# A shift moved from a row of maxima into the exponential's bias, and one cast moved from VectorE to ScalarE, in an attention and retention block

## Chip, cores and metric

The kernel runs on one core of a Trainium2 chip. The metric is the device time of one execution in microseconds (us), the median of several runs. TensorE (PE) multiplies matrices and writes to PSUM, VectorE (DVE) and ScalarE (ACT) read PSUM and SBUF, GpSimd (POOL) works on SBUF alone, and SyncE (SP) issues the DMAs. Each engine runs its own instructions in program order and waits on semaphores for the others.

## What is computed

A block of a streaming encoder over 4096 positions of width 1024: an RMS norm, one input projection, two groups of heads, a gated mix, an output projection, a second norm and the residual sum. The first group is forgetting attention, 8 heads of width 64; the second is chunkwise retention, 4 heads of width 128. What the change touches is the softmax of the attention:

```python
logits = jnp.einsum('bhqd,bhkd->bhqk', qb, kb) * scale
logits = logits + c[:, :, q0:q1, None] - c[:, :, None, :q1]
logits = jnp.where(kpos <= qpos, logits, -jnp.inf)
p = jax.nn.softmax(logits, axis=-1)
outs.append(jnp.einsum('bhqk,bhkd->bhqd', p.astype(vb.dtype), vb))
```

A softmax does not change when one constant is added to all logits of a row. The kernel subtracts a rough maximum of each row and adds a constant shift, so that the exponentials fit their 16-bit type.

## The kernel before

**Stages.** `phase_f0` (0 to about 425 us) norms the input, splits it into two 16-bit parts and projects the first four attention heads. Then `attention` runs over 64 items, one per head and block of 512 queries (`items`, head by head, 8 blocks each). Beside it run the fillers (`fill_f1`, `fill_r` twice, `fill_o`): the projections of the other heads, the retention and the output projection. A loop at the end of the kernel interleaves the two by their costs. After the last item `fill_o` runs alone to the end.

**A step of attention.** An item has 4 to 32 steps, one per 128 keys; over all items that is 1152. In a step TensorE forms 128 x 512 logits in a PSUM bank with two matmuls (the first also adds the row's negative maximum, which lies as rows 0 to 16 of the tile `xq`). ScalarE takes the exponential twice, in float32 (`pf`, line 1132) and in float16 (`ph`, line 1133), both with the scale `es`, an operand of one value per partition from the tile `gsc`. GpSimd forms the rest `pl = pf - ph` (line 308). The step then waits in the list `pvq`; `emit_pv` multiplies `ph` and `pl` by the values, four steps at a time, once at least six are queued.

**Maxima.** `max_tile` forms one tile of logits a second time, 128 queries by 512 keys, without the forget terms, and VectorE takes the maximum along the keys (line 999, tile `mrow`): 1152 tiles too. With the last tile of an item `max_row` starts. It reduces to one value per query (line 1011, tile `m4`, named `sm` in the trace), adds the shift (a `tensor_scalar` at line 144), waits `MAGE` ticks, transposes on TensorE (line 1017), lets ScalarE cast the coarse part (`mr[:, 0]`, line 1019), lets VectorE form what is left (line 147) and cast it as the second part (`mr[:, 1]`, line 144), and sends both through DRAM (`MR`) into `xq`.

**What sets the order.** The order on every queue is written by the program: each helper is a generator that is resumed once per `tick()`, and a `yield` inside it moves what follows one tick later. Ticks come with every step of attention and every step of a filler. Line 144 is the helper `ts`, line 141 `tt`, line 147 `stt`, line 308 the GpSimd helper, line 104 `mm` and line 107 the DMA helper, so tiles tell instructions apart better than lines. All PSUM tiles share one pool of 8 banks.

```python
        yield 1
        ts(m4, m4, gsc[items[n][0] // 4][0][:, KT + 5 : KT + 6], None, ALU.add, ALU.bypass)
        for _ in range(MAGE):
            yield 1
```

Of the kernel before, what the change touches and what calls it, by code (L numbers as in the profile page):

```python
# [12 lines left out]
AF = mybir.ActivationFunctionType  # L13
ALU = mybir.AluOpType
# [3 lines left out]
KT = 8  # L18
# [2 lines left out]
NEG = -1.0e30  # L21
NORM_EPS = 1e-6
GN_EPS = 1e-5
PSHIFT = 24.0
CP = 16
R1 = CP + 1
R2 = R1 + CP + 2
TOP, MID, LOW = 2.0**15, 2.0**9, 2.0**-2
# [25 lines left out]
def kernel(  # L54
# [14 lines left out]
    nc = tc.nc  # L69
# [18 lines left out]
    def SB(tag, shape, dt=F32):  # L88
        cnt[0] += 1
        slot = SHARED.get(tag, tag)  # L90
        return sbp.tile(shape, dt, tag=slot, name=f"{tag}_{cnt[0]}", bufs=BUFS.get(slot, 1))

    def PS():
        cnt[0] += 1
        return psp.tile([128, 512], F32, tag="ps", name=f"ps_{cnt[0]}", bufs=8)
# [7 lines left out]
    def mm(o, lhsT, rhs, start, stop):  # L103
        nc.tensor.matmul(out=o, lhsT=lhsT, rhs=rhs, start=start, stop=stop, skip_group_check=True)  # L104

    def dma(o, i):
        nc.sync.dma_start(out=o, in_=i)  # L107
# [18 lines left out]
    def until(key):  # L126

        while key not in done:
            assert chains, key
            tick()  # L130
# [9 lines left out]
    def tt(o, a, b, op):  # L140
        nc.vector.tensor_tensor(out=o, in0=a, in1=b, op=op)  # L141

    def ts(o, a, s1, s2, op0, op1):
        nc.vector.tensor_scalar(out=o, in0=a, scalar1=s1, scalar2=s2, op0=op0, op1=op1)  # L144

    def stt(o, a, s, b, op0, op1):
        nc.vector.scalar_tensor_tensor(out=o, in0=a, scalar=s, in1=b, op0=op0, op1=op1)  # L147
# [24 lines left out]
    gain = SB("gain", [128, KT])  # L172
    fbb = SB("fbb", [128, FH])
    nhalf = SB("nhalf", [128, 4])
    gsc = [[SB(f"gsc{g}{part}", [128, KT + 8]) for part in range(2)] for g in range(5)]
    state = [SB(f"state{h}", [128, 5, 128]) for h in range(2)]

# [49 lines left out]
    def w_scale(g, parts, mk, age=VAGE):  # L227

        n = KT * len(parts)
        m1 = SB("sm", [128, 1])  # L230
        if g < 4:
            for i in range(len(parts)):
                tt(mk[:, i * KT : (i + 1) * KT], mk[:, i * KT : (i + 1) * KT], gain, ALU.mult)
        nc.vector.tensor_reduce(out=m1, in_=mk[:, 0:n], axis=AX.X, op=ALU.max, apply_absolute_value=True)
        for _ in range(age):
            yield 1
        p = PS()
        nc.tensor.transpose(p[0:1, 0:128], m1, idf)
        m2 = SB("sm", [1, 1])
        nc.vector.tensor_reduce(out=m2, in_=p[0:1, 0:128], axis=AX.X, op=ALU.max)  # L240
        ts(m2, m2, 1e-6, 1.0 / 8192.0, ALU.max, ALU.mult)
        for _ in range(age):
            yield 1
        p2 = PS()
        mm(p2[:, 0:1], tri[0:1, :], m2, True, True)
        sc = SB("sm", [128, 1])
        nc.vector.reciprocal(out=sc, in_=p2[:, 0:1])
        for part in parts:
            f = gsc[g][part]
            if g < 4:  # L250
                ts(f[:, 0:KT], gain, sc[:, 0:1], None, ALU.mult, ALU.bypass)
            else:
                ts(f[:, 0:KT], gain, 0.0, sc[:, 0:1], ALU.mult, ALU.add)
            ts(f[:, KT : KT + 1], p2[:, 0:1], 1.0 / 512.0, None, ALU.mult, ALU.bypass)
        yield 1
        for part in parts:
            f = gsc[g][part]
            ts(f[:, KT + 1 : KT + 2], f[:, KT : KT + 1], 0.5, None, ALU.mult, ALU.bypass)
            if g < 2 and part == 0:


                ts(f[:, KT + 3 : KT + 4], sc, 1.0 / 512.0, 16.0, ALU.mult, ALU.min)
                tt(f[:, KT + 2 : KT + 3], f[:, KT + 3 : KT + 4], f[:, KT : KT + 1], ALU.mult)
                tt(f[:, KT + 3 : KT + 4], f[:, KT + 3 : KT + 4], f[:, KT + 3 : KT + 4], ALU.mult)
                ts(f[:, KT + 5 : KT + 6], f[:, KT + 3 : KT + 4], PSHIFT, None, ALU.mult, ALU.bypass)
                ts(f[:, KT + 6 : KT + 7], f[:, KT + 3 : KT + 4], 8.0, None, ALU.mult, ALU.bypass)
                ts(f[:, KT + 7 : KT + 8], f[:, KT + 3 : KT + 4], -8.0, None, ALU.mult, ALU.bypass)
                nc.vector.reciprocal(out=f[:, KT + 4 : KT + 5], in_=f[:, KT + 6 : KT + 7])
            elif g < 4:
                stt(f[:, KT + 2 : KT + 3], f[:, KT : KT + 1], 131072.0, f[:, KT : KT + 1], ALU.mult, ALU.mult)  # L270
            else:
                ts(f[:, KT + 2 : KT + 3], sc, 1.0, None, ALU.mult, ALU.bypass)
            done.add(("ws", g, part))
# [264 lines left out]

    def phase_f0():
        nc.vector.memset(nhalf, -0.5)  # L540
        wu = SB("z1", [128, 512], BF16)
        nc.gpsimd.memset(wu, 0.0)
        xs = a_load(0, 0, 2, "xt")
# [366 lines left out]
    items = [(h, qb) for h in range(FH) for qb in range(NB)]  # L910
# [98 lines left out]
    def max_row(n, xq, mrow, qb):  # L1009
        m4 = SB("sm", [128, 4])  # L1010
        nc.vector.tensor_reduce(out=m4, in_=mrow[:, :, 0 : qb + 1], axis=AX.X, op=ALU.max, negate=True)
        yield 1
        ts(m4, m4, gsc[items[n][0] // 4][0][:, KT + 5 : KT + 6], None, ALU.add, ALU.bypass)
        for _ in range(MAGE):
            yield 1
        p = PS()
        nc.tensor.transpose(p[0:4, 0:128], m4, idf)
        mr = SB("mr", [4, 2, 128], F16)
        nc.scalar.activation(out=mr[:, 0, :], in_=p[0:4, 0:128], func=AF.Copy, scale=1.0 / (TOP * CP))
        yield 1  # L1020
        r = SB("sm", [4, 128])
        stt(r, mr[:, 0, :], -TOP * CP, p[0:4, 0:128], ALU.mult, ALU.add)
        ts(mr[:, 1, :], r, 1.0 / MID, None, ALU.mult, ALU.bypass)
        for _ in range(3):
            yield 1
        dma(MR[n].rearrange("w (t p) -> t w p", p=128), mr)
        for _ in range(4):
            yield 1
        dma(xq[0:CP, :], MR[n][0:1, :].to_broadcast([CP, 512]))
        dma(xq[CP:R1, :], MR[n][1:2, :])  # L1030
        done.add(("m", n))
# [3 lines left out]
    def attention():  # L1035
# [65 lines left out]
        for n, (h, qb) in enumerate(items):  # L1101
            xq = xqs.pop(n)
            lq, z = lqs.pop(n)
            it = dict(n=n, z=z)
            es = gsc[h // 4][0][:, KT + 4 : KT + 5]
            until(("m", n))
            steps = 4 * (qb + 1)
            for kt in range(steps):
                c, kk = kt // 4, kt % 4
                kc, vt = get_chunk(h, c)  # L1110
                chunks_use[n, kt] = (kc, vt)
                cost = 0.0
                if kt % 2 == 0:
                    if kt % 4 == 2 and len(pvq) >= 6:
                        for _ in range(4):
                            cost += 88 * (4 - max(0, pvq[0][2]))
                            emit_pv()
                    sts = []
                    for j in (kt - 4 * qb, kt + 1 - 4 * qb):
                        p = PS()  # L1120
                        if j >= 0:
                            mm(p[:, j * 128 : (j + 1) * 128], idb, maskT, True, False)
                        sts.append(p)
                i = kt - 4 * qb
                q0 = max(0, i) * 128
                st = sts[kt % 2]
                mm(st[:, q0:512], kc[0 : R2 + 64, 1, kk * 128 : (kk + 1) * 128], xq[0 : R2 + 64, q0:512], i < 0, False)
                mm(st[:, q0:512], kc[:, 0, kk * 128 : (kk + 1) * 128], lq[:, q0:512], False, True)
                pf = SB("pf", [128, 512])
                ph = SB("ph", [128, 512], F16)  # L1130
                pl = SB("pl", [128, 512], F16)
                nc.scalar.activation(out=pf[:, q0:512], in_=st[:, q0:512], func=AF.Exp, scale=es)  # L1132
                nc.scalar.activation(out=ph[:, q0:512], in_=st[:, q0:512], func=AF.Exp, scale=es)  # L1133
                ptt(pl[:, q0:512], pf[:, q0:512], ph[:, q0:512], ALU.subtract)
                pvq.append((it, kt, i, ph, pl, kt == 0, kt == steps - 1))
                cost += 2 * (512 - q0) * 0.42 + (56 if i >= 0 else 0)
                gstep[0] += 1
                for _ in range(max_rate(gstep[0])):
                    if max_ready():
                        max_tile()  # L1140
                        cost += 216
                yield cost
            drain(max_tiles(n + 1))
            load_x(n + 4)
            load_lq(n + 2)
# [219 lines left out]
```

## Time and profile before

| what | value |
|---|---|
| median of 3 runs | 3148.3 us (3146.62 to 3150.13) |
| the profiled execution's own time | 3151.84 us |
| its span, first to last instruction | 3150.0 us |
| TensorE busy | 3029.2 us (96%) |
| VectorE busy | 2076.8 us (66%) |
| ScalarE busy | 1873.1 us (59%) |
| GpSimd busy | 1351.6 us (43%) |
| mean granted TensorE clock | 0.985 |

Busy time is the union of an engine's instructions; the busy sums of groups count overlapping instructions twice. "Idle before, releaser" names the engine whose result ended the wait. The chain that ended last follows the program back from its last instruction, at each step to what released it.

### The profile page before, as it was taken

To read this page: it belongs to the slowest core of one execution; us is meant where nothing else is said; L and a number is where in the kernel's file an instruction comes from. 1 tells how busy PE (TensorE), PEld (TensorE's weight loads), DVE (VectorE), ACT (ScalarE), POOL (GpSimd) and SP (SyncE) were. 2 spreads that over 40 slices of the span, in tenths; PEclk is the share of its full clock that TensorE was granted. 3 is DMA by queue.
4 is the path that set the end of the run, shared out by engine and by line. 5 is a ranking of instruction groups with operands and counts; after the bars stand their busy time and mean duration, and the time that the engine had idled before them with its cause. 6 is when DMAs were issued, how large, how long until landed. Compare 5 with 4: busy or idle time off the path is not lost.

```text
span 3150.0 us, 67744 instructions
## 1 busy us (share of the span) xinstructions
PE 3029.2 (96%) x26798; PEld 1794.7 (57%) x26799; DVE 2076.8 (66%) x4372; ACT 1873.1 (59%) x3508; POOL 1351.6 (43%) x1285
## 2 busy tenths in 40 slices
PE   8999989999999999999999999999999999889999
PEld 6666555555555555665555565556556555555554
DVE  6545567446455676777678878776877786645555
ACT  4333345676677667666667675667666766653332
POOL 0000024554555455555545564556455645540000
PEclk9999999999999999999999999999999999999999
DMA  6455753223235231311114223112111321124443
GB/s 179 156 166 152 199 123 95 67 82 93 69 88 134 64 80 35 91 51 52 55 57 101 58 71 97 51 43 78 49 51 45 111 73 33 57 68 141 141 141 120
DMA packets 266174, 284.62 MB, mean 90 GB/s; under 512 B 58976, under 2 KB 212192, under 8 KB 265856
## 3 DMA queue, kind: packets, MB, share of 16 engines
q1 hardware_dynamic: 265856, 280.30, 31.3%
q8 instruction: 210, 3.44, 0.4%
q14 instruction: 108, 0.88, 0.1%
HBM read 194.88 MB, written 88.74 MB: 90 GB/s over the span
## 4 chain that ended last, share of the span: by engine, by line
PE 80%; DVE 12%; ACT 3%; issue 2%; DMA 2%; POOL 1%; SPq 1%; POOLq 0%; DVEq 0%; ACTq 0%
PE ps L104 77%; DVE mrow L999 3%; DVE s L141 2%; DVE s L144 1%; DVE sm L141 1%; DMA rw<-in_w_in_dram 1%; ACT ph L1133 1%; PE ps L1188 1%; ACT pf L1132 1%; SPq L107 1%; PE ps L349 1%; DVE sm L144 1%; DVE s L147 1%; POOL pl L308 1%; POOL sm L308 0%
## 5 line engine op out<-in xcount | busy, mean ns | idle before, releaser
L308 POOL TENSOR_TENSOR pl<-pf,ph 128x512 f16<-128x512 f32 (+3 forms) x1152 | 1281.2, 1117 | 1135.0 <-ACT ph L1133 856.8
L1132 ACT ACTIVATE pf<-ps,gsc 128x512 f32<-128x512 f32 (+3 forms) x1152 | 758.2, 658 | 694.0 <-PE ps L104 677.0
L999 DVE TENSOR_REDUCE mrow<-ps 128x1 f32<-128x512 f32 (+3 forms) x1152 | 717.6, 641 | 356.9 <-PE ps L104 345.8
L104 PE MATMUL ps<-wn,xh 128*128 128x512 f16 (+2 forms) x3840 | 852.7, 359 | 3.1 <-DVE qk L147 2.9
L1133 ACT ACTIVATE ph<-ps,gsc 128x512 f16<-128x512 f32 (+3 forms) x1152 | 754.3, 655 | 0.0
L104 PEld LDWEIGHTS <-xh 128*128 128x128 f16 x4608 | 450.2, 98 | 450.5 <-issue 22.5
L104 PE MATMUL ps<-xh,wt 128*128 128x512 f16 x2688 | 667.7, 381 | 3.4 <-DVE mrow L999 2.0
L104 PEld LDWEIGHTS <-wt 128*128 128x128 f16 x3168 | 308.9, 98 | 356.4 <-issue 24.6
L104 PEld LDWEIGHTS <-ph 128*128 128x128 f16 x8448 | 423.9, 97 | 76.0 <-issue 8.0
L104 PE MATMUL ps<-vt,ph 128*128 128x65 f16 (+1 forms) x8448 | 433.8, 195 | 10.4 <-ACT ph L1133 7.3
L104 PE MATMUL ps<-xq,kc 99*128 99x512 f16 (+3 forms) x1152 | 420.0, 365 | 14.6 <-DMA xq<-MR 9.7
L104 PE MATMUL ps<-vt,pl 128*128 128x65 f16 x4224 | 423.4, 193 | 3.8 <-POOL pl L308 3.8
L104 PE MATMUL ps<-lq,kc 128*128 128x512 f16 (+3 forms) x1152 | 419.1, 364 | 0.0
L104 PE MATMUL ps<-kc,xq 99*128 99x512 f16 (+3 forms) x1152 | 383.1, 364 | 34.3 <-DVE mrow L999 25.1
L104 PEld LDWEIGHTS <-pl 128*128 128x128 f16 x4224 | 393.3, 99 | 5.1 <-POOL pl L308 4.7
L104 PEld LDWEIGHTS <-kc 128*128 128x128 f16 (+1 forms) x3072 | 281.9, 99 | 196.8 <-issue 22.2
L141 DVE TENSOR_TENSOR s<-s,s 64x512 f32<-64x512 f32 (+1 forms) x256 | 258.6, 1010 | 33.3 <-ACT s L755 26.3
L308 POOL TENSOR_TENSOR sm<-sm,nhalf 128x4 f32<-128x4 f32 (+2 forms) x80 | 63.0, 787 | 350.5 <-DVE sm L144 308.5
L104 PEld LDWEIGHTS <-xq 99*128 99x128 f16 x1152 | 112.3, 98 | 139.4 <-issue 9.5
L104 PE MATMUL ps<-wt,xh 128*128 128x512 f16 x768 | 184.0, 381 | 0.0
L141 DVE TENSOR_TENSOR ps<-ps,maskM 128x128 f32<-128x128 f32 x256 | 75.1, 293 | 108.4 <-PE ps L104 107.6
L141 DVE TENSOR_TENSOR xh<-ps,xh 128x256 f16<-128x256 f32 (+1 forms) x128 | 70.3, 555 | 105.5 <-ACT xh L338 86.1
(120 smaller groups left out, 2525.2 us busy)
## 6 DMA issues: line engine op xcount, KB each, us to landing
xh<-XT SPq DMA_DIRECT2D x176, 256.0 KB
rw<-in_w_in_dram SPq DMA_DIRECT2D x104, 256.0 KB
xt<-in_x_dram SPq DMA_DIRECT2D x36, 512.0 KB
s<-MX SPq DMA_DIRECT2D x32, 512.0 KB
out_dram<-xt SPq DMA_DIRECT2D x31, 512.0 KB
s<-in_x_dram SPq DMA_DIRECT2D x28, 512.0 KB
VD<-s SPq DMA_DIRECT2D x16, 516.0 KB
vt<-VD SPq DMA_DIRECT2D x64, 129.0 KB
```

Of the source, the lines that this page charges most:

```text
L104: nc.tensor.matmul(out=o, lhsT=lhsT, rhs=rhs, start=start, stop=stop, skip_group_check=True)
L107: nc.sync.dma_start(out=o, in_=i)
L141: nc.vector.tensor_tensor(out=o, in0=a, in1=b, op=op)
L144: nc.vector.tensor_scalar(out=o, in0=a, scalar1=s1, scalar2=s2, op0=op0, op1=op1)
L147: nc.vector.scalar_tensor_tensor(out=o, in0=a, scalar=s, in1=b, op0=op0, op1=op1)
L308: nc.gpsimd.tensor_tensor(out=o, in0=a, in1=b, op=op)
L349: nc.tensor.transpose(p[:, t * 128 : (t + 1) * 128], xs[t][:, k * 128 : (k + 1) * 128], idf)
L999: nc.vector.tensor_reduce(out=mrow[:, t, c : c + 1], in_=p[:, 0:w], axis=AX.X, op=ALU.max)
L1132: nc.scalar.activation(out=pf[:, q0:512], in_=st[:, q0:512], func=AF.Exp, scale=es)
L1133: nc.scalar.activation(out=ph[:, q0:512], in_=st[:, q0:512], func=AF.Exp, scale=es)
L1188: nc.tensor.transpose(p[:, e * 128 : (e + 1) * 128], mxt[:, half * 4 + e, :], idf)
```

## The change

The shift is no longer added to the maxima on VectorE. It becomes the bias of both exponentials, as a tile `shift` of one value per partition; since the bias is added after the scale, its value is 3.0 where 24.0, times a factor of the scale, stood before. The column of `gsc` that held the scaled shift is dropped, and so are one tick before the transposition's wait and the `tensor_scalar` that followed it. The second part of the row of maxima is cast by ScalarE from the tile `r`, one tick after VectorE has formed `r`; the DMA behind it keeps its tick.

```diff
-PSHIFT = 24.0
+PSHIFT = 3.0
...
+    shift = SB("shift", [128, 1])
...
-                ts(f[:, KT + 5 : KT + 6], f[:, KT + 3 : KT + 4], PSHIFT, None, ALU.mult, ALU.bypass)
...
+        nc.vector.memset(shift, PSHIFT)
...
         nc.vector.tensor_reduce(out=m4, in_=mrow[:, :, 0 : qb + 1], axis=AX.X, op=ALU.max, negate=True)
-        yield 1
-        ts(m4, m4, gsc[items[n][0] // 4][0][:, KT + 5 : KT + 6], None, ALU.add, ALU.bypass)
         for _ in range(MAGE):
             yield 1
...
         stt(r, mr[:, 0, :], -TOP * CP, p[0:4, 0:128], ALU.mult, ALU.add)
-        ts(mr[:, 1, :], r, 1.0 / MID, None, ALU.mult, ALU.bypass)
+        yield 1
+        nc.scalar.activation(out=mr[:, 1, :], in_=r, func=AF.Copy, scale=1.0 / MID)
...
-                nc.scalar.activation(out=pf[:, q0:512], in_=st[:, q0:512], func=AF.Exp, scale=es)
-                nc.scalar.activation(out=ph[:, q0:512], in_=st[:, q0:512], func=AF.Exp, scale=es)
+                nc.scalar.activation(out=pf[:, q0:512], in_=st[:, q0:512], func=AF.Exp, bias=shift, scale=es)
+                nc.scalar.activation(out=ph[:, q0:512], in_=st[:, q0:512], func=AF.Exp, bias=shift, scale=es)
```

How the order moves, at one item (the 33rd of 64, at about 1523 us). On VectorE before, the subtraction that forms `r` (a `SCALAR_TENSOR_TENSOR` from `mr`) and the cast into `mr` stand together between two maxima:

```order
L999 TENSOR_REDUCE mrow_22702<-ps_22727 128x1
L147 SCALAR_TENSOR_TENSOR s_4385_22584<-s_4385_22584,s_3933_20334 128x512
L999 TENSOR_REDUCE mrow_22702<-ps_22744 128x1
L147 SCALAR_TENSOR_TENSOR sm_22752<-mr_22750,ps_22748 4x128
L144 TENSOR_SCALAR mr_22750<-sm_22752 4x128
L999 TENSOR_REDUCE mrow_22702<-ps_22816 128x1
```

The same place after the change:

```order
L1000 TENSOR_REDUCE mrow_22669<-ps_22694 128x1
L147 SCALAR_TENSOR_TENSOR s_4388_22556<-s_4388_22556,s_3934_20305 128x512
L1000 TENSOR_REDUCE mrow_22669<-ps_22715 128x1
L147 SCALAR_TENSOR_TENSOR sm_22719<-mr_22702,ps_22700 4x128
L1000 TENSOR_REDUCE mrow_22669<-ps_22783 128x1
```

The cast is gone from VectorE, and the subtraction stands where it stood. On ScalarE before, one cast (into `mr` from PSUM) stands between two pairs of exponentials:

```order
L1132 ACTIVATE pf_22738<-ps_22718,gsc_8_150 128x512
L1133 ACTIVATE ph_22739<-ps_22718,gsc_8_150 128x512
L1019 ACTIVATE mr_22750<-ps_22748 4x128
L1132 ACTIVATE pf_22810<-ps_22806,gsc_8_150 128x512
L1133 ACTIVATE ph_22811<-ps_22806,gsc_8_150 128x512
L850 ACTIVATE s_4251_21917<-ps_22670,gsc_13_155 128x256
```

After the change:

```order
L1018 ACTIVATE mr_22702<-ps_22700 4x128
L1132 ACTIVATE pf_22709<-ps_22685,shift_150,gsc_9_151 128x512
L1133 ACTIVATE ph_22710<-ps_22685,shift_150,gsc_9_151 128x512
L1023 ACTIVATE mr_22702<-sm_22719 4x128
L1132 ACTIVATE pf_22777<-ps_22773,shift_150,gsc_9_151 128x512
L1133 ACTIVATE ph_22778<-ps_22773,shift_150,gsc_9_151 128x512
```

The first cast has moved ahead of a pair of exponentials, a second cast that reads VectorE's `sm_22719` stands behind that pair, and every exponential has `shift` as a further input.

Over the whole program VectorE loses 64 additions to `m4` and 64 casts, and ScalarE gains 64 casts. The order on SyncE and GpSimd is the same row for row. On TensorE nothing moves but the transpositions of line 1017, some of which come one tick earlier.

## Rows read from the trace of the kernel before

**Rows 1.** The page's first part: busy time, share of the span, instructions.

```profile
PE 3029.2 (96%) x26798; PEld 1794.7 (57%) x26799; DVE 2076.8 (66%) x4372; ACT 1873.1 (59%) x3508; POOL 1351.6 (43%) x1285
```

**Rows 2.** Instructions of line 1132, with min/median/max ns; and a window's busy time per engine.

```profile
L1132 ACT ACTIVATE pf<-ps,gsc x1152: 342/687/860, 424.8 to 2813.8; 128x512 f32<-128x512 f32 x192
...
1500.00:2000.00 500.00, 474.24 (x4579) 285.02 (x4578) 385.23 (x753) 331.63 (x614) 270.29 (x242) 0.98 0.26 73
```

**Rows 3.** The chain that ended last, whole span, by line.

```profile
by line: PE ps L104 77.4%; DVE mrow L999 2.8%; issue 2.1%; DVE s L141 2.0%; DVE s L144 1.4%; DVE sm L141 1.1%; DMA rw<-in_w_in_dram 1.1%; ACT ph L1133 0.9%; PE ps L1188 0.9%; ACT pf L1132 0.9%; SPq L107 0.8%; PE ps L349 0.8%; DVE sm L144 0.
```

**Rows 4.** Waits over the whole span: us in total, times, longest us.

```profile
ACT pf L1132 <- PE ps L104: 677.0, 575, 7.3
...
PE ps L104 <- DVE mrow L999: 34.5, 37, 4.2
...
PE ps L104 <- ACT ph L1133: 8.8, 3, 3.9
```

**Rows 5.** ScalarE's groups by shape: count, busy us, mean ns, idle before.

```profile
L1132 ACT ACTIVATE pf<-ps,gsc 128x512 f32<-128x512 f32 x960 | 665.5, 693 | 556.6 <-PE ps L104 543.4 <-issue 2.4 <-POOL pl L308 2.1
...
L755 ACT ACTIVATE s<-ps,gsc 128x512 f32<-128x512 f32 x64 | 44.4, 694 | 5.2 <-PE ps L104 5.2
...
L850 ACT ACTIVATE s<-ps,gsc 128x256 f32<-128x256 f32 x64 | 30.8, 482 | 4.7 <-PE ps L104 4.6
...
L420 ACT ACTIVATE s<-ps 128x256 f16<-128x256 f32 x64 | 25.0, 390 | 41.3 <-PE ps L104 41.3
...
L845 ACT COPY s<-ps 128x512 f32<-128x512 f32 x32 | 18.9, 591 | 0.0
...
L1019 ACT ACTIVATE mr<-ps 4x128 f16<-4x128 f32 x64 | 16.2, 253 | 5.9 <-PE ps L1017 5.7
```

**Rows 6.** ScalarE in order of time near 2767 us: start, duration, instruction.

```profile
2766.27 0.67 ACT L1132 ACTIVATE pf<-ps,gsc 128x512 f32<-128x512 f32 x1
2766.84 0.68 ACT L1133 ACTIVATE ph<-ps,gsc 128x512 f16<-128x512 f32 x1
2767.41 0.58 ACT L833 COPY s<-ps 128x512 f32<-128x512 f32 x1
2767.87 0.71 ACT L1132 ACTIVATE pf<-ps,gsc 128x512 f32<-128x512 f32 x1
```

**Rows 7.** VectorE's groups by shape that hold the removed instructions.

```profile
L144 DVE TENSOR_SCALAR sm<-sm,gsc 128x4 f32<-128x4 f32 x128 | 61.1, 478 | 3.1
...
L144 DVE TENSOR_SCALAR mr<-sm 4x128 f16<-4x128 f32 x64 | 32.7, 511 | 2.3 <-DVE sm L147 0.2
```

**Rows 8.** The same instructions by tile: min/median/max ns, first and last start.

```profile
L144 DVE TENSOR_SCALAR sm<-sm,gsc x160: 210/229/1228, 408.0 to 3124.2; 128x4 f32<-128x4 f32 x128, 128x1 f32<-128x1 f32 x32
...
L144 DVE TENSOR_SCALAR mr<-sm x64: 214/272/1080, 413.4 to 2732.7; 4x128 f16<-4x128 f32 x64
```

**Rows 9.** Pieces of the chain that are removed instructions: start, us, what.

```profile
1508.89 1.23 DVE sm L144
...
2724.45 1.14 DVE sm L144
```

**Rows 10.** ScalarE's first cast and VectorE's subtraction behind it, three items.

```profile
1154.98 0.27 ACT L1019 ACTIVATE mr<-ps 4x128 f16<-4x128 f32 x1
...
1160.54 0.27 DVE L147 SCALAR_TENSOR_TENSOR sm<-mr,ps 4x128 f32<-4x128 f16 x1
...
1523.10 0.25 ACT L1019 ACTIVATE mr<-ps 4x128 f16<-4x128 f32 x1
1524.82 0.69 ACT L1132 ACTIVATE pf<-ps,gsc 128x512 f32<-128x512 f32 x1 [1.47 <-PE ps L104]
...
1528.39 0.26 DVE L147 SCALAR_TENSOR_TENSOR sm<-mr,ps 4x128 f32<-4x128 f16 x1
...
1935.05 0.25 ACT L1019 ACTIVATE mr<-ps 4x128 f16<-4x128 f32 x1
...
1940.30 0.27 DVE L147 SCALAR_TENSOR_TENSOR sm<-mr,ps 4x128 f32<-4x128 f16 x1
```

## The prediction, made before the changed kernel ran

> **What bounds the kernel now.** I read the page's first part, then the chain that ended last, then the waits, then the groups of the engines that the change touches. TensorE is busy 3029 us of a span of 3150 [rows 1], and 77% of the chain is its matmuls [rows 3]: the kernel is bound by TensorE, and time is gained or lost only where TensorE waits. The steps of attention, 1152 of them, run from 424.8 to 2813.8 us [rows 2], one in 2.07 us on average. In them ScalarE mostly waits for TensorE: 677 us before 575 of the 1152 first exponentials, 1.18 us each, while TensorE waited for an exponential directly only three times, 8.8 us in all [rows 4]. Even between 1500 and 2000 us ScalarE is busy 332 us of 500 [rows 2]. So ScalarE has room, but it isn't off the chain: the exponentials hold 0.9% + 0.9% of it [rows 3], 57 us of 3150, where a delay on ScalarE goes through GpSimd's rest or a PSUM bank back to TensorE. VectorE is the engine that TensorE waits for most: 34.5 us in 37 places, for the maxima [rows 4].
>
> **The change, part by part.**
>
> *The bias of the exponentials.* 2304 exponentials gain a second operand of one value per partition. The trace of before shows no activation with a bias tile, so I bound its price. The nearest rows are activations with and without the first such operand, the scale: 694 against 591 ns for 128 x 512 and 482 against 390 ns for 128 x 256 [rows 5], 92 to 103 ns. The spacing in a busy stretch tells the same: exponentials with a scale tile start 0.57 us apart, the copy without one takes 0.46 us of the engine's time [rows 6], 0.11 us less. The lower bound is nothing, if the engine reads both operands at once; below nothing is excluded, since the instruction only gets an input more. The upper is 0.11 us. I take 0.10, because the operand added is of the same kind as the one in those rows, and nothing in the trace shows two read at once. The Trainium skill ("ScalarE: Activation LUTs", section on what ACT_TABLE_LOAD costs) says that an ACTIVATE takes 186 ns and 0.833 ns an element with immediates, and that each pointer operand of [128,1] adds about 93 ns, bias and scale alike. By that rule the term below would be 98 x 0.093 = 9.1 us, and with a bias that is free it would be 0; the rows above agree with it for the scale, and no row shows the bias.
>
> On ScalarE that is 2304 x 0.10 = 230 us more. Most of it is hidden: two pairs bring 0.4 us between idle times of 1.18 us [rows 4]. What isn't hidden is what lies on the chain: 57 us at 0.575 us each [rows 3, 6] are 98 exponentials, and 98 x 0.10 gives **+10 us**. Ends: 0 if the bias is free, 230 if nothing hides it; the value lies near the low end since TensorE stays the bound in almost every stretch.
>
> *The addition to `m4` removed, 64 on VectorE.* They share a row with 64 others of the same form: 61.1 us for 128, so about 30 us. *The cast into `mr` removed, 64 on VectorE*: 32.7 us [rows 7]. Medians are 229 and 272 ns, the longest 1228 and 1080 [rows 8]; the long ones, near one GpSimd instruction long, are waits beside a busy GpSimd. Beside the chain these 63 us are worth nothing, since VectorE idles for a third of the span. Of the 128, 15 lie on the chain with 8.0 us: six long ones of 0.9 to 1.2 us, from 1508.89 to 2724.45 us [rows 9], and nine that make 1.7 us together. The whole is the most that can be had, 0 the least. I take **-5 us**: behind each the next maximum or a fellow wait for GpSimd comes shortly after. What is late next is VectorE itself, with the 34.5 us of maxima, of which these 15 are a small part.
>
> *The cast on ScalarE, 64 more.* Its twin takes 253 ns from PSUM [rows 5]; 64 x 0.25 = 16 us of ScalarE, of which the share that the exponentials have on the chain (98 of 2304, 4%) makes **+0.7 us**. That it waits matters more. Its input is VectorE's subtraction, and ScalarE runs in order: while VectorE is late, the exponentials behind the cast stand still, and with them GpSimd's rests and the products by the values. Before, the subtraction came over 3 us after the end of the cast it reads in 10 of 64 items, all between 1155 and 1941 us, by 3.4 to 6.4 us: 5.3 us in the first, 5.0 in the one of the order above and 5.0 in the last [rows 10]. The ten make 49 us. After the change ScalarE reaches the new cast about one pair of exponentials after the first, 1.15 us and the cast's 0.25 later, so it would stand some 49 - 14 = 35 us in these ten. The cover: six steps queue in `pvq` before four are multiplied, 4 us or more at 2.07 us a step, eight banks, and ScalarE's own idle time, such as the 1.47 us right behind the cast at 1523 us [rows 10]. Ends: 0, and 27 us if in each of ten places 2.7 us get through. I take **+4 us**: half the places, under 1 us each, as TensorE is seldom hurt by ScalarE today [rows 4].
>
> *Edits with one answer.* The memset of `shift` and the dropped column of `gsc` are three VectorE instructions that run once: 0. The transposition one tick earlier is TensorE work that only moves; SyncE's and GpSimd's orders are unchanged; SyncE's DMA of `mr` keeps its place and its tick, and waits for ScalarE instead of VectorE; what it brings is wanted an item later: 0.
>
> **Sum.** +10 - 5 + 0.7 + 4 = +9.7 us on the profiled execution's own time of 3151.84 us: 3161.5. That execution lies 3.5 us above the median of the three runs, 3148.3, so the forecast for the median is **3158 us**, 0.3% slower.
>
> **The rivals.**
>
> *Absorbed.* The bias costs nothing, or ScalarE's idle time takes it even on the chain. For it: 677 us of waiting for TensorE [rows 4]. Against it: 57 us of chain run through exponentials, back to back at 0.57 us [rows 3, 6]. It gives 3148.3 - 5 + 4.7 = 3148 us.
>
> *Faster: VectorE was the engine to relieve.* Where VectorE is late, each removed wait beside GpSimd lets the next maximum free its bank sooner. All 8 us of the chain go [rows 9], and half of the 37 waits for maxima shorten by a removed instruction's median, 37 / 2 x 0.23 = 4 us [rows 4, 8], while the bias stays hidden: 3148.3 - 12 = 3136 us. It decides once the exponentials cost less than 0.02 us each on the chain (98 x 0.02 = 2 us) and the new cast finds its input ready. Against it stand the two prices above.
>
> *ScalarE stands behind VectorE.* The ten waits get through to TensorE, 27 us, beside the 10 us of the bias, with 2 us given back: 3148.3 + 35 = 3183 us. For it: TensorE already idles 26 us between 1500 and 2000 us [rows 2], so both engines are tight there. Against it: the six queued steps.
>
> **How the numbers follow.** Forecast 0.50, absorbed 0.25, faster 0.12, ScalarE behind VectorE 0.13. A measurement of this kernel tells about 0.2%, 6.3 us, from no change. The forecast's own range is 3151 to 3170; 0.07 of its chance lies within 0.2%. Slower: 0.43 + 0.13 = 0.56. Within 0.2%: 0.07 + 0.21 of the absorbed case = 0.28. Faster: 0.12 + 0.04 = 0.16. The range reaches down to the absorbed case with all 8 us of relief, 3148.3 - 8 = 3140, and up to 14 us of bias (more exponentials coming onto the chain) and 12 of stalls, 3148.3 + 26 = 3174. Outside lie half of the faster case and the last rival, under 0.2 together.
>
> **What would show it.** In the profile of the changed kernel: the groups of lines 1132 and 1133 near 790 ns for 128 x 512 instead of 693 (near 693, the bias is free); ScalarE busy about 2090 us; lines 1132 and 1133 with a larger share of the chain, above 65 us; VectorE about 60 us less busy, and the wait of TensorE for maxima near 30 us; a new row in which ScalarE waits for VectorE's subtraction, 30 to 60 us. The forecast is wrong if the exponentials keep their duration, if TensorE's waits for ScalarE and GpSimd don't grow, or if the maxima's 34.5 us fall by more than half.

## The result and the profile after

The changed kernel takes **3169.8 us** in the median of four runs (3166.8 to 3170.7), the kernel before beside it 3148.9 us (3146.6 to 3150.1): a ratio of 1.0062, with a 95% interval of 1.0049 to 1.0074. It is slower by 20.9 us. The forecast was slower, 3158 us, within 3140 to 3174; the direction and the range held; the size, 9.7 us, was less than half of the 20.9 that came.

The profiled execution has a span of 3168.9 us. The first part of its page, beside [rows 1]:

```profile
PE 3029.2 (96%) x26799; PEld 1792.8 (57%) x26799; DVE 2023.7 (64%) x4243; ACT 2067.5 (65%) x3572; POOL 1346.0 (42%) x1285
```

TensorE's busy time is the same to the tenth. The span grew by 18.9 us, so all of it is idle time of TensorE. ScalarE has 194.4 us more work, VectorE 53.1 us less. ScalarE's groups by shape (count, busy us, mean ns of one, idle before), beside [rows 5]:

```profile
L1132 ACT ACTIVATE pf<-ps,shift,gsc 128x512 f32<-128x512 f32 x960 | 753.2, 785 | 401.4 <-PE ps L104 384.7 <-POOL pl L308 8.8 <-issue 2.1
L1133 ACT ACTIVATE ph<-ps,shift,gsc 128x512 f16<-128x512 f32 x960 | 751.0, 782 | 0.0
...
L1023 ACT ACTIVATE mr<-sm 4x128 f16<-4x128 f32 x64 | 19.2, 301 | 37.1 <-DVE sm L147 36.8
```

An exponential of 128 x 512 takes 785 ns instead of 693: the bias tile costs 92 ns. The new cast takes 301 ns, where the prediction took 250 from its twin, and ScalarE stands 36.8 us for VectorE's subtraction ahead of it, in 27 places, where the prediction worked out 35 us in ten. The waits (us in total, times, longest us), beside [rows 4]:

```profile
ACT pf L1132 <- PE ps L104: 486.1, 443, 7.4
...
DVE sm L141 <- POOL sm L308: 42.0, 35, 3.0
PE ps L104 <- DVE mrow L1000: 41.9, 41, 4.6
ACT mr L1023 <- DVE sm L147: 36.8, 27, 4.5
...
PE ps L104 <- ACT ph L1133: 11.4, 4, 4.8
...
PE ps L104 <- POOL pl L308: 9.0, 15, 1.1
```

TensorE's wait for VectorE's maxima did not fall to 30 us but rose from 34.5 to 41.9, although VectorE has less to do. And the chain that ended last, by line, beside [rows 3]:

```profile
by line: PE ps L104 73.3%; DVE mrow L1000 3.1%; issue 2.7%; DVE s L141 2.2%; DVE s L144 1.7%; ACT pf L1132 1.6%; ACT ph L1133 1.6%; POOL pl L308 1.4%; DVE sm L141 1.1%; SPq L107 1.1%; DMA rw<-in_w_in_dram 1.0%; PE ps L1188 0.9%; PE ps L349 
```

The exponentials hold 1.6% + 1.6% of 3168.9, 101 us, where they held 57; TensorE's main row fell from 77.4% to 73.3%.

Where in the program the idle time lies is read from windows, cut at the first exponential of the fifth of the eight heads, item 33 (1601 us before, 1599 us after). The columns are the stretch, its length, busy us of PE, PEld, DVE, ACT, POOL, then TensorE's granted clock as a share of full speed, the busy share of the DMA engines and their GB/s. Before:

```profile
425.00:1601.00 1176.00, 1149.95 (x11092) 658.59 (x11090) 749.08 (x1495) 789.19 (x1445) 641.83 (x592) 0.99 0.29 77
1601.00:2814.00 1213.00, 1147.62 (x11254) 691.27 (x11253) 907.12 (x1766) 819.67 (x1508) 673.70 (x603) 0.98 0.22 65
```

After:

```profile
427.00:1599.00 1172.00, 1146.21 (x11093) 656.27 (x11092) 720.16 (x1428) 885.66 (x1479) 639.98 (x592) 1.00 0.29 77
1599.00:2833.00 1234.00, 1151.39 (x11253) 691.99 (x11251) 883.71 (x1708) 916.85 (x1536) 669.59 (x603) 0.98 0.22 64
```

The first half is no longer than before, though ScalarE has 96 us more to do in it; TensorE idles 1176.00 - 1149.95 = 26 us before and 26 us after. The second half is 21 us longer: TensorE idles 65.4 us before and 82.6 after, and is busy 4 us longer. ScalarE's load does not tell the halves apart, since after the change it is busy 76% of the first and 74% of the second; VectorE's does, 61% against 72%. By what TensorE waited for in the second half, before:

```profile
PE ps L104 <- DVE mrow L999: 27.5, 26, 4.2
...
PE ps L104 <- ACT ph L1133: 7.3, 2, 3.9
...
PE ps L104 <- POOL pl L308: 3.7, 5, 1.0
```

and after:

```profile
PE ps L104 <- DVE mrow L1000: 31.8, 29, 4.6
PE ps L104 <- ACT ph L1133: 11.4, 4, 4.8
...
PE ps L104 <- POOL pl L308: 7.2, 13, 1.0
...
PE ps L812 <- DVE mrow L1000: 2.8, 1, 2.8
```

The maxima's banks (+4.3, and +1.9 in the last row, which was 0.9 at line 811 before), the exponentials (+4.1) and GpSimd's rests (+3.5) make 13.8 of the 17.2 us.

A correction to the text ahead of the prediction: the maxima's tiles are not formed "without the forget terms". Their one matmul takes the rows of `xq` and `kc` that hold these terms; only the second matmul, with the low parts of queries and keys, is left out. No number hung on it.

### The profile page after: what moved, and what is told of

Same layout as the page of the kernel before. It is cut to its first block, busy times and chain, and to the rows that moved or that the text cites. A ratio compares the mean times of both kernels' runs of the same rounds, so it can differ in the third digit from the quotient of the medians.

```text
span 3168.9 us, 67652 instructions
## 1 busy us (share of the span) xinstructions
PE 3029.2 (96%) x26799; PEld 1792.8 (57%) x26799; DVE 2023.7 (64%) x4243; ACT 2067.5 (65%) x3572; POOL 1346.0 (42%) x1285
## 4 chain that ended last, share of the span: by engine, by line
PE 75%; DVE 12%; ACT 4%; issue 3%; DMA 2%; POOL 2%; SPq 1%; POOLq 0%; DVEq 0%; ACTq 0%
PE ps L104 73%; DVE mrow L1000 3%; DVE s L141 2%; DVE s L144 2%; ACT pf L1132 2%; ACT ph L1133 2%; POOL pl L308 1%; DVE sm L141 1%; SPq L107 1%; DMA rw<-in_w_in_dram 1%; PE ps L1188 1%; PE ps L349 1%; DVE s L147 1%; DVE sm L144 1%; POOL sm L308 0%
## 5 line engine op out<-in xcount | busy, mean ns | idle before, releaser
L1132 ACT ACTIVATE pf<-ps,shift,gsc 128x512 f32<-128x512 f32 (+3 forms) x1152 | 863.2, 749 | 505.1 <-PE ps L104 486.1
L1133 ACT ACTIVATE ph<-ps,shift,gsc 128x512 f16<-128x512 f32 (+3 forms) x1152 | 860.5, 747 | 0.0
```

## The experiments

The theories held against each other: that the exponentials' operand makes the loss (theory A, the forecast's main term); that the new cast on ScalarE, in order behind VectorE, makes it; and, of the gain, that VectorE's relief is worth several us, or nothing (theory N). Later runs ask where the loss arises (theories C and D) and by what way it reaches TensorE (P and Q). Each text on record names those it tells apart. All results (us, medians; the kernel before was measured beside each run, on the same chip):

| run | what it is | us | before | ratio, 95% interval |
|---|---|---|---|---|
| e1_zero_bias | before, with a bias tile of zeros | 3168.5 | 3151.3 | 1.0054 [1.0042, 1.0067] |
| e2_cast_alone | before, with the cast on ScalarE | 3151.4 | 3151.3 | 0.9999 [0.9990, 1.0007] |
| e3_immediate_bias | after, bias a constant | 3150.3 | 3151.3 | 0.9993 [0.9984, 1.0002] |
| e4_cast_back | after, cast back on VectorE | 3173.7 | 3151.3 | 1.0069 [1.0055, 1.0083] |
| e5_first_half | after, tile in items 1 to 32 only | 3149.2 | 3151.5 | 0.9992 [0.9983, 1.0002] |
| e6_second_half | after, tile in items 33 to 64 only | 3173.0 | 3151.5 | 1.0069 [1.0055, 1.0083] |
| e7_m4_relief_alone | constant bias, cast on VectorE | 3153.8 | 3151.5 | 1.0007 [0.9998, 1.0016] |
| e8_no_shift_no_cast | constant bias, no cast at all | 3149.7 | 3151.5 | 0.9997 [0.9988, 1.0006] |
| e9_norm_later | after, norm's use of the power later | 3120.5 | 3153.1 | 0.9900 [0.9886, 0.9913] |
| e10_norm_later_const | e3 with the same | 3108.1 | 3153.1 | 0.9862 [0.9847, 0.9877] |
| e11_pf_only | after, tile on `pf` only | 3173.5 | 3153.1 | 1.0068 [1.0055, 1.0081] |
| e12_no_cast_norm_later | e8 with the same | 3107.2 | 3153.1 | 0.9860 [0.9847, 0.9874] |

The kernel before moved from 3148.9 to 3153.1 us between these groups of runs, so a difference in us between runs of different groups, such as one from the changed kernel's 3169.8, is known to about 4 us.

**The operand alone**, e1_zero_bias, against the kernel before (a tile of zeros, so the arithmetic is that of before):

```diff
+    shift = SB("shift", [128, 1])
+        nc.vector.memset(shift, 0.0)
-                nc.scalar.activation(out=pf[...], in_=st[...], func=AF.Exp, scale=es)
+                nc.scalar.activation(out=pf[...], in_=st[...], func=AF.Exp, bias=shift, scale=es)
```

and likewise for `ph`.

> The kernel before, with one edit: both exponentials get a bias tile of zeros; the shift stays on VectorE, the cast stays on VectorE. Theory A (the operand itself is the loss, about 92 ns on each of 2304 exponentials, and its share on the chain is larger than forecast): 3148.9 + 16 to 24 us, 3165 to 3173, with exponentials of 128 x 512 near 785 ns. Theory B (the loss is the cast that waits for VectorE on ScalarE, the operand is mostly hidden): at most 3148.9 + 6, 3155 or less, with the same 785 ns.

Measured: 17.2 us slower, most of the loss of 20.9, with nothing else changed; the intervals of the two ratios overlap. TensorE's wait for the maxima is 44.1 us in 39 places in this run.

**The cast alone**, e2_cast_alone, against the kernel before:

```diff
-        ts(mr[:, 1, :], r, 1.0 / MID, None, ALU.mult, ALU.bypass)
+        yield 1
+        nc.scalar.activation(out=mr[:, 1, :], in_=r, func=AF.Copy, scale=1.0 / MID)
```

> The kernel before, with one edit: the second part of the row of maxima is cast by ScalarE one tick after VectorE's subtraction; shift and exponentials as before. Theory A: 3148.9 plus or minus 5 us, since ScalarE's wait of some 35 us in about 27 places is covered and 32 us of VectorE are given back. Theory B: 3148.9 + 12 to 20, 3161 to 3169, with ScalarE's wait for the subtraction turning up as waits of TensorE.

Measured: no difference, 0.1 us. The wait is there, 42.8 us in 24 places, and VectorE's wait for the power and TensorE's for the maxima are those of before, within 1.4 us:

```profile
ACT mr L1024 <- DVE sm L147: 42.8, 24, 5.0
DVE sm L141 <- POOL sm L308: 35.4, 34, 3.2
PE ps L104 <- DVE mrow L999: 33.1, 37, 4.2
```

So nothing of it that can be told reaches TensorE, and the cast's wait is no cause. Six queued steps and ScalarE's idle time, the cover that the prediction named, fit this; no run takes them away.

**The shift as a constant**, e3_immediate_bias, against the changed kernel:

```diff
-    shift = SB("shift", [128, 1])
-        nc.vector.memset(shift, PSHIFT)
-                nc.scalar.activation(out=pf[...], ..., func=AF.Exp, bias=shift, scale=es)
+                nc.scalar.activation(out=pf[...], ..., func=AF.Exp, bias=PSHIFT, scale=es)
```

> The changed kernel, with one edit: the bias 3.0 is a constant in the instruction in place of a tile. Theory A: exponentials back at 693 ns and the time at 3142 to 3151 us, since all that cost is gone and the relief of VectorE stays. Theory B: 3158 to 3168 us, since the cast on ScalarE stays. If a constant bias costs as much as a tile, the exponentials stay near 785 ns and the time near 3170 under both.

Measured: the loss is gone, 19.5 us below the changed kernel, and level with before. The same two groups of exponentials:

```profile
L1130 ACT ACTIVATE pf<-ps,gsc 128x512 f32<-128x512 f32 x960 | 663.7, 691 | 515.5 <-PE ps L104 501.6 <-POOL pl L307 2.9 <-issue 2.4
L1131 ACT ACTIVATE ph<-ps,gsc 128x512 f16<-128x512 f32 x960 | 659.8, 687 | 0.0
```

691 ns with a constant bias, 693 with none, 785 with a tile. The Trainium skill ("ScalarE: Activation LUTs", section on what ACT_TABLE_LOAD costs) gives a price for an ACTIVATE with immediate scale and bias, and adds about 93 ns for each pointer operand. The rows agree with 94 ns, and show of the bias what the trace of before could not.

**The cast put back**, e4_cast_back, against the changed kernel:

```diff
+        ts(mr[:, 1, :], r, 1.0 / MID, None, ALU.mult, ALU.bypass)
         yield 1
-        nc.scalar.activation(out=mr[:, 1, :], in_=r, func=AF.Copy, scale=1.0 / MID)
```

> The changed kernel, with one edit: the cast of the second part goes back to VectorE, behind its subtraction. Theory A: 3163 to 3171 us, little changed. Theory B: 3149 to 3156 us, since the wait of ScalarE for VectorE (36.8 us in 27 places) is gone.

Measured: 3173.7 us, nothing regained (theory A named 3171 at most). With e2 this clears the cast from both sides: it does nothing without the operand, and its removal does nothing beside it.

**Which half**, e5_first_half and e6_second_half, against the changed kernel, for e6 with `n >= 32`:

```diff
-                ... func=AF.Exp, bias=shift, scale=es)
+                ... func=AF.Exp, bias=shift if n < 32 else PSHIFT, scale=es)
```

> The changed kernel with the bias as a tile in items 0 to 31 only (576 of 1152 steps, to about 1600 us) and as a constant in items 32 to 63. Run with the constant everywhere: 3150.3 us; with the tile everywhere: 3169.8. Theory C (the operand costs time where VectorE is busiest, beside retention and output projection, since there the chain of waits runs through ScalarE and GpSimd into VectorE's norms): 3150 to 3155 us. Theory D (each exponential costs its share wherever it stands): near 3160 us.

> The changed kernel with the bias as a tile in items 32 to 63 only. Theory C: 3164 to 3171 us. Theory D: near 3160 us. If C holds, this and the run with the tile in the first half add up to the 19.5 us between constant and tile everywhere.

Measured: the tile in the first half costs nothing (3149.2 us, against 3150.3 with no tile), the tile in the second half costs everything (3173.0). Each half adds the same 1152 operands. So the place counts, as theory C has it, though the two times lie 1 and 2 us outside its ranges; theory D's 3160 is out in both. One stretch in which the second half's operands lie on the chain is e6's at 2310 us (start us, us, what):

```profile
2310.66 0.78 ACT pf L1132
2311.44 0.67 ACT ph L1133
2312.11 0.46 ACT pf L1132
2312.66 0.78 ACT ph L1133
2313.45 0.17 ACT mr L1023
2313.62 0.47 ACT s L846
2314.08 0.68 ACT pf L1132
...
2316.69 0.78 ACT pf L1132
2317.47 0.68 ACT ph L1133
2318.18 0.98 POOL sm L308
2319.18 1.12 DVE sm L141
...
2320.93 2.75 DVE s L144 x4
2323.70 0.69 DVE s L147
2324.39 0.61 DVE mrow L1000
2325.05 30.41 PE ps L104 x303
```

Five pairs of exponentials run without a gap (a cast and a copy between the second and the third), then the power of a retention norm on GpSimd, the norm on VectorE, and only then the maximum whose bank TensorE wants. In e3, without the tile, the same five pairs on ScalarE's timeline:

```profile
2295.20 0.69 ACT L1130 ACTIVATE pf<-ps,gsc 128x512 f32<-128x512 f32 x1
...
2296.36 0.69 ACT L1130 ACTIVATE pf<-ps,gsc 128x512 f32<-128x512 f32 x1
...
2299.31 0.66 ACT L1130 ACTIVATE pf<-ps,gsc 128x512 f32<-128x512 f32 x1
...
2301.23 0.69 ACT L1130 ACTIVATE pf<-ps,gsc 128x512 f32<-128x512 f32 x1 [0.69 <-PE ps L104]
```

Pairs start 1.16 us apart instead of 1.34 (2310.66 and 2312.00 in e6's timeline), and before the fifth ScalarE has caught up and waits 0.69 us for TensorE. With the tile it has not caught up. From the first of these exponentials to the start of the power it takes 7.48 us in e6 and 6.92 in e3, so the power comes 0.56 us later; VectorE stands 0.53 us for it in both. Summed over the program this way is thin. From item 33 on, VectorE waits for the power 26.2 us in e3 and 28.6 in the changed kernel, and 26.3 in e11 (below), which is as slow; TensorE waits for the maxima 26.7, 31.8 and 31.5 us. These norms run from 1188.5 us on, by the trace of the changed kernel, and of the 128 instructions below 36 start before 1600 us and 92 after, so most of them stand in the second half:

```profile
L775 DVE BATCH_NORM_STATS2 sm<-s x128: 261/276/297, 1188.5 to 2797.8; 128x6 f32<-128x128 f32 x128
```

**VectorE's relief alone**, e7_m4_relief_alone (the edits of e3 and e4 together) and e8_no_shift_no_cast. In e8 the subtraction writes the second part itself, in 16 bits, and the row of `aux` that multiplied it by `MID` holds ones instead; the sum in the logits is the same. Against e3's kernel:

```diff
-        r = SB("sm", [4, 128])
-        stt(r, mr[:, 0, :], -TOP * CP, p[0:4, 0:128], ALU.mult, ALU.add)
+        stt(mr[:, 1, :], mr[:, 0, :], -TOP * CP, p[0:4, 0:128], ALU.mult, ALU.add)
         yield 1
-        nc.scalar.activation(out=mr[:, 1, :], in_=r, func=AF.Copy, scale=1.0 / MID)
...
-    aux[0:CP], aux[CP] = TOP, MID
+    aux[0:CP], aux[CP] = TOP, 1.0
```

> The kernel before without the addition to the maxima: the shift is a constant bias of the exponentials, the cast stays on VectorE. It is the first half of the relief by itself, 30 us of VectorE in 64 instructions. Theory R (what leaves the chain is gained, as forecast): 3145 to 3150 us. Theory N (VectorE's time isn't worth anything here, the next wait takes over): 3150 to 3153 us, the same as before.

> A version meant to beat both: constant bias, and VectorE's subtraction writes the second part of the row of maxima itself, without the factor 1/512 and with a row of ones where the row of 512 stood, so that neither engine has a cast. VectorE loses 128 instructions (63 us) and ScalarE gains none. Theory R: 3143 to 3148 us, 4 to 5 us under the run with constant bias and the cast on ScalarE. Theory N: 3149 to 3152 us.

Measured: 3153.8 and 3149.7 against 3151.5, both within what can be told from no change (e7 is 0.8 us above theory N's range); e8's interval leaves at most 0.12%, 3.8 us, for the relief. e8's page shows what was taken off VectorE, beside [rows 1], 46.8 us, with ScalarE as before:

```profile
PE 3032.0 (96%) x26798; PEld 1796.5 (57%) x26799; DVE 2030.0 (64%) x4242; ACT 1874.1 (60%) x3508; POOL 1352.1 (43%) x1285
```

So 46.8 us of VectorE's work, with no operand and no cast to pay for it, buy nothing that can be told.

**Half of the operands**, e11_pf_only, against the changed kernel:

```diff
-                nc.scalar.activation(out=ph[...], ..., func=AF.Exp, bias=shift, scale=es)
+                nc.scalar.activation(out=ph[...], ..., func=AF.Exp, bias=PSHIFT, scale=es)
```

> The changed kernel with the bias as a tile in the float32 exponential and as a constant in the float16 one: half of the operands, spread over all steps. If each operand costs its share: 3160 us, plus or minus 3. If slack takes the first part and only the second hurts: 3150 to 3155.

Measured: 3173.5 us, as slow as with all of them (ratios 1.0068 and 1.0062), which neither case of the text had. `pf` takes 783 ns, `ph` 688. Half the operands cost no less than all: the loss is not so much per operand. From item 33 on TensorE idles 65.4 us in e3, 78.9 in this run and 82.6 in the changed kernel, so by idle time half of the operands make 13.5 of 17.2 us. The rest of this run's loss there is TensorE's own: busy 1155 us at a granted clock of 0.97, where e3 has 1148 and the changed kernel 1151, both at 0.98.

**The norm's use of the power, later**, e9_norm_later, against the changed kernel (the generator of the norm waits four more ticks between GpSimd's power and VectorE's first use of it), e10_norm_later_const with e3's constant beside it, and e12_no_cast_norm_later with e8's edits beside it:

```diff
-    def rstd_of(ss, n, scale, eps, up=1.0):
+    def rstd_of(ss, n, scale, eps, up=1.0, more=0):
...
         ptt(r, v, nhalf[:, 0:n], ALU.pow)
         yield 1
         yield 1
+        for _ in range(more):
+            yield 1
...
-        r = yield from rstd_of(mv[:, :, 1], 4, 1.0, epsp[:, h : h + 1])
+        r = yield from rstd_of(mv[:, :, 1], 4, 1.0, epsp[:, h : h + 1], more=4)
```

> The changed kernel, with one edit: in the group norm of the retention, four more ticks between GpSimd's power and VectorE's use of it. Theory P (the loss reaches TensorE through GpSimd: the power stands behind rests that wait for slower exponentials, VectorE waits for the power, and the maxima behind it free their banks late): 3153 to 3162 us, half or more of the 19.5 us gone, and TensorE's wait for maxima (41.9 us) down by 5 us or more. Theory Q (the power isn't the way; VectorE or the banks are late for other reasons): 3167 to 3172 us.

> The same edit on the version with a constant bias (3150.3 us), so that what the edit does by itself is known. Theory P: 3145 to 3151 us, at most 5 us gained, as there the power is seldom late. Theory Q: 3148 to 3153 us. Whatever it is, the gain in the changed kernel counts only as far as it exceeds this one.

> The version with a constant bias and no cast (3149.7 us), with the later use of the power. Theory P: 3143 to 3149 us. Theory Q: 3148 to 3153 us.

Measured: the changed kernel gains 49 us, the one with the constant 42 us and e8's version 43 us. All three texts missed: far more was gained than the path was thought to be worth. In e9's trace TensorE, ScalarE and GpSimd have the same order as in the changed kernel, row for row; only VectorE's and SyncE's differ. Two waits of e3:

```profile
DVE sm L141 <- POOL sm L307: 37.1, 33, 3.3
PE ps L104 <- DVE mrow L998: 33.4, 40, 4.2
```

and e10's:

```profile
DVE sm L141 <- POOL sm L307: 17.5, 16, 2.8
PE ps L104 <- DVE mrow L1000: 13.2, 26, 1.6
PE ps L104 <- ACT ph L1133: 9.8, 4, 3.9
```

VectorE's wait for the power, 37.1 us in e3, is 17.5, and TensorE's wait for the maxima falls from 33.4 to 13.2. The operand still costs 3120.5 - 3108.1 = 12.4 us, against 17.2 (e1) to 19.5 without the delay, so 5 to 7 us of it are gone. By TensorE's idle time from item 33 on it costs 17.2 us without the delay (82.6 against 65.4) and 9.3 with it (51.0 in e9, 41.7 in e10). The versions of e10 and e12 beat both kernels, e12 with 0.9860 [0.9847, 0.9874].

## Why the prediction was right in direction and short in size

- *The operand's price*, 0.10 us: right, a little high. 92 ns by the rows of the same shape, 785 against 693, and ScalarE's busy time rose to 2067.5 us where about 2090 was named.
- *What of it gets through*, 98 exponentials on the chain by 0.10 us, +10: this is **the term that was mis-sized**. It measured +17.2 alone (e1) and 19.5 on top of the other edits (after against e3). The step that failed is to count the exponentials on the old chain and let each bring its own price. The first half's operands bring nothing, the second half's everything (e5, e6), and one operand of each pair nearly as much as two (e11). The exponentials' chain time grew by 44 us, not by 10, and the span by 18.9: pieces that lay on TensorE's row before lie on ScalarE's now. In the one stretch that was followed it comes where ScalarE no longer catches up in a burst; what was on the chain before did not tell of it.
- *The addition and the cast taken off VectorE*, -5: **failed**. e7, e8 and e3 all equal the kernel before, with 14, 47 and 51 us less on VectorE. Fifteen instructions with 8.0 us on the chain [rows 9] were worth nothing that can be measured, and e8's interval excludes 5 us. That something stands close behind each, as the text feared ("the next maximum or a fellow wait for GpSimd comes shortly after"), fits this and is not shown.
- *The cast on ScalarE*, +0.7: nothing that shows (e2), and *its wait*, +4: **failed**. The wait is real, 36.8 us where 35 was worked out, though in 27 places and not in ten, and nothing of it reaches TensorE (e2, e4).
- The sum of +9.7 was thus a term half as large as it is, and three (-5, +0.7, +4) that nearly cancel and are each 0 as far as can be told. That the range held is in part luck: it rests on its upper end, where "14 us of bias" and 12 of stalls were allowed for; the stalls did not come, and the bias went past its 14.
- *The rivals.* Absorbed: true of the first half alone. Faster, VectorE to relieve: refuted by e7 and e8 even where the operand is free. ScalarE behind VectorE: its time, 3183, was about as far off as the forecast's, but its mechanism, the cast's wait, is refuted by e2. Its remark that TensorE already idles where both engines are tight was the better lead: the half that pays is the one in which TensorE idled 65 us before, against 26 in the other.
- *What would show it.* Five of six signs came: exponentials near 790 ns, ScalarE's busy time, more than 65 us of them on the chain, VectorE 53 us lighter, a wait for the subtraction of 30 to 60. The sixth, TensorE's wait for maxima near 30 us, came out at 41.9, and was the one that told of the missing part.
- *"Time is gained or lost only where TensorE waits"*: so here, where TensorE is busy 3029.2 us before and after, but not in every run. e10's TensorE has the same work and is busy 13 us less from item 33 on.

Shown: the operand tile makes the loss (e1, e3), in the second half (e5, e6), and none of the other edits does anything by itself that can be told. Shown: with the norm's power used four ticks later the kernel is some 42 us faster, and VectorE's wait for the power and TensorE's for the maxima are shorter. That edit also moves what follows the power on VectorE; no run parts the shorter wait from the moved order. Argued only, from one stretch, and against the sums over the program, which hardly differ: that the burst of exponentials delays GpSimd and with it the power. Open: by what way the operand's other 12.4 us reach TensorE, and why half the operands cost nearly as much as all; no run here tells it.

## What to carry to other kernels

A constant belongs in an activation as a constant, not as a tile: here that is 691 against 785 ns on each of 1920 instructions of 128 x 512, and 20 us of 3150. An operand's price must be placed by stage: idle time that hides it in one half of a program says nothing of the half in which the bound engine already stands, and chain time counted before the change (57 us of exponentials) is no measure of what will lie on the chain after it (101). Where an in-order engine waits for another's short result, moving the use a few steps later may be worth more than taking work off that engine; 47 us of VectorE's work bought nothing that can be told here, four ticks bought 1.4%.

## What was not expected of the hardware

- A constant bias on an exponential costs nothing beside none (691 and 693 ns), and the tile's price hardly depends on the width: 785 ns in the changed kernel against 691 with the constant for 128 x 512, 467 against 371 for 128 x 128.
- VectorE's work taken out beside a busy GpSimd gave nothing back: additions of the removed form took from 210 to 1228 ns [rows 8], yet leaving 64 of them out moved no end; what waits in their place no run names. The Trainium skill ("Perfetto Trace Analysis", section on optimizing Scalar/DVE operations) says that offloading some work to ScalarE may make sense if VectorE is saturated. Here VectorE was busy 66%, and moving the cast brought nothing (e2).
- Delaying the use of a result shortened the program: in e10 the stretch from item 33 on takes 1176 us instead of 1213 before. TensorE idles 41.7 us instead of 65.4 in it, and is also busy 13 us less, at a mean granted clock of 0.99 of full speed (2.4 GHz) instead of 0.98:

```profile
1593.00:2769.00 1176.00, 1134.33 (x11250) 686.70 (x11249) 871.88 (x1708) 823.09 (x1535) 677.67 (x603) 0.99 0.23 67
```
